# Where tiles lie in SBUF: the streamed operands of each stage moved down behind the weights, x and the small tiles moved to the upper end

## The chip, the cores and the metric

The kernel runs on one core of one Trainium2 chip. The metric is the device time of one execution in microseconds (us). Three executions of the kernel before gave 2356.27, 2360.15 and 2360.02, with a median of 2360.02.

## What is computed

512 tokens of 1024 features in float32 go through two blocks. Cut to what matters (`x` is carried through all of it, each line with its own weights):

```python
x = x + 0.5 * ffn(rms_norm(x))           # swiglu: (silu(h @ Wg) * (h @ Wu)) @ Wo, 1024 -> 2816 -> 1024
x = x + mixer1(rms_norm(x)) @ Wmo        # band attention and sparse attention, heads of 64
x = x + 0.5 * ffn(rms_norm(x))           # a second swiglu
x = x + mixer2(rms_norm(x))              # GLA (4 heads) and retention (4 heads), each with an output
                                         # projection ya or yb, then one more projection
x = x + moe(rms_norm(x))                 # 32 experts of float32 weights, 64 places each; RMS norm at the end
```

## The kernel before

The activations are kept transposed: eight tiles of 128 features x 512 tokens. The five stages run one after the other in one program: `ffn`, `mixer1`, `ffn`, `mixer2`, `moe`.

**The large matmuls.** Up to the experts every large product is made of three matmuls in float32r. Each operand is split into a high and a low part: ACT makes the high part (line 84), DVE the low part (line 85). `mm3` then adds high·high (line 99), high weight·low activation (line 100) and low weight·high activation (line 101) into one PSUM tile. In `gemm` the weight part is the stationary operand (loaded by LDWEIGHTS as 128x128) and the activation part is the moving operand, 128x512, streamed from SBUF through the array. A trace row such as `po<-hh,whi` reads: PSUM tile po, moving hh, stationary whi. The exception is `vv`, in which the weights whi and wlo are the moving operand.

**What is streamed where.** The names are needed below:
- `xh`, `xl`: the parts of the normalised x, moving in all projections `pg`, `pu` (ffn) and `pj` (mixers). At the end of mixer2 the same places are used again for `oh`, `ol`, which move in the last projection, also called `po` in rows.
- `hh`, `hl`: the parts of the hidden tiles of `ffn`, moving in `po`. `ffn` goes through the 22 hidden tiles in three parts of 8, 7 and 7 (PARTS). In each part `pg` and `pu` of every hidden tile are made and then eight `po` sums over the part's tiles: 24 x (8 + 7 + 7) = 528 matmuls of po in each ffn.
- `fh`, `fl`: the parts of a half of mixer2's heads, moving in `ya` (GLA) and `yb` (retention).
- `mh`, `ml`: the parts of the second half of mixer1's result, moving in mixer1's `po`.
- `th`, `tlo`: the parts of transposed attention weights, moving in mixer1's `pv`; `sh`, `sl` and `rh`, `rl` do the like for short sums of mixer2 (`pvo`, `rs`).
- `wexp`: float32 weights of the experts, moving in the experts' `pg`, `pu`, `pd`. They are held in a ring of 21 places at the upper end of SBUF, in the places of wraw, whi and wlo (`EXTRA`), and in a few late ones.

**What sets the order of the work.** The code is issued in program order on each engine. `load_w` puts each weight tile on SP's DMA queue (line 91) into one of three `wraw` places; a DMA whose place is still in use waits in that queue, and whatever is queued behind it on SP waits too. Which earlier instruction a new tile has to wait for is set by the place: a tile waits for the last users of the places that it covers. So moving a pool can move a wait even when no operation changes.

**Where tiles lie.** Pools are stacked from the lower end (left) and from the upper end (right). Before, the left side holds const, wraw, whi, wlo, xhl (xh and xl), `small`, then x, and behind x the pools of the stage. All parts of SBUF below are given per partition.

Of the kernel before, what the change touches and what calls it, by code (L numbers as in the profile page):

```python
# [10 lines left out]
F32R = mybir.dt.float32r  # L11
# [24 lines left out]
def ap_of(t, offset, dims):  # L36
    return bass.AP(tensor=t.tensor, offset=t.offset + offset, ap=dims)


class Kern:  # L40
    def __init__(self, ctx, tc, A, out, dbg=None, stop=None):
        self.ctx, self.tc, self.nc, self.A, self.out = ctx, tc, tc.nc, A, out
        self.dbg = dbg or {}
        self.stop = stop
        self.sin = None
        e = ctx.enter_context
        self.const = e(tc.tile_pool(name="const", bufs=1))
        self.wp = e(tc.tile_pool(name="wts", bufs=1))
        self.xp = e(tc.tile_pool(name="xhl", bufs=1))
        self.sm = e(tc.tile_pool(name="small", bufs=2))  # L50
        self.dram = e(tc.tile_pool(name="dram", bufs=1, space=bass.MemoryType.DRAM))
        self.ps = e(tc.tile_pool(name="psum", bufs=1, space=PSUM))
        self.xd = self.dram.tile([128, DT, 512], F32, name="xd")
# [2 lines left out]
        return self.tc.alloc_tile_pool(name=name, bufs=bufs, side=side, reuse_waits="tile")  # L56

    def open_x(self):
        self.xpool = self.pool("x")
        self.x = [self.xpool.tile([128, 512], F32, name=f"x{t}") for t in range(DT)]  # L60

    def spill(self, t):
# [148 lines left out]
    def ffn(self, w_in, w_out, nxt, aside=()):  # L211
        nc, A, X = self.nc, self.A, self.X
        aside = list(aside)
        if True:
            fp = self.pool("ffn")
            for pi, (n0, cnt) in enumerate(PARTS):
                if pi == len(PARTS) - 1 and nxt is not None:
                    nxt = nxt()
                H = []
                for n in range(n0, n0 + cnt):  # L220
                    if n != 1:
                        wg, self.first = self.first or self.load_w(A[w_in][:, n, 0]), None
                        pg = self.acc("pg")
                    wu = self.load_w(A[w_in][:, n, 1])
                    if n == 1:
                        pg = pg1
                        pu = self.ps.tile([128, 512], F32, name="pu", tag="lg", bufs=2)
                    else:
                        self.gemm(pg, wg, X, DT)
                        pu = self.acc("pu")  # L230
                    if n == 0:

                        self.gemm(pu, wu, X, DT)
                        wg, pg1 = self.load_w(A[w_in][:, 1, 0]), self.acc("pg")
                        self.gemm(pg1, wg, X, DT, range(4))
                        self.norm_end()
                        self.gemm(pg1, wg, X, DT, range(4, DT))
                    if n >= 3 and aside:
                        aside.pop(0)()
                    g = fp.tile([128, 512], F32, name="g", bufs=2)  # L240
                    nc.vector.tensor_tensor(out=g, in0=pg, in1=self.rstd, op=OP.mult)
                    nc.scalar.activation(g, g, AF.Silu)
                    if n:
                        self.gemm(pu, wu, X, DT)
                    u = fp.tile([128, 512], F32, name="u", bufs=2)
                    nc.vector.tensor_tensor(out=u, in0=pu, in1=self.rstd, op=OP.mult)
                    h = fp.tile([128, 512], F32, name="h", bufs=2)
                    nc.vector.tensor_tensor(out=h, in0=g, in1=u, op=OP.mult)
                    hh = fp.tile([128, 512], F32R, name="hh", bufs=10)
                    hl = fp.tile([128, 512], F32R, name="hl", bufs=10)  # L250
                    self.split(h, hh, hl)
                    H.append((hh, hl))
                for n in range(DT):
                    w = self.load_w(A[w_out][:, n, n0 * 128:(n0 + cnt) * 128])
                    po = self.acc("po")
                    self.gemm(po, w, H, cnt)
                    nc.vector.scalar_tensor_tensor(self.x[n], po, 0.5, self.x[n], op0=OP.mult, op1=OP.add)
                    if pi == len(PARTS) - 1 and nxt is not None:
                        nxt(n)
            fp.release()  # L260


    def bias_lines(self):
# [387 lines left out]
    def mixer1(self, nxt):  # L651
        nc, A = self.nc, self.A
        self.xpool.release()
        mp = self.mp = self.pool("mixp")
        self.ms = self.pool("mixs", 2)
        mw = self.mw = self.pool("mixw", 2)
        self.sk = mp.tile([128, 2, 8], F32, name="sk")
        nc.sync.dma_start(self.sk[:, 0], ap_of(A["sinks"], 0, [[0, 128], [1, 8]]))
        nc.vector.tensor_scalar(self.sk[:, 1], self.sk[:, 0], -1.0, None, op0=OP.mult)
        self.mix = mp.tile([128, DT, 512], F32, name="mix")  # L660
        self.qs = ([], [])
        self.pvq = []
        ps = self.proj(4)
        self.norm_end(tokens=True)
        pq = [self.proj(n) for n in range(2)]
        self.ka = self.k_tile(4, "k_norm_a", "ka", ps)
        for n in range(2):
            self.q_tile(n, "q_norm_a", self.qs[0], pq[n])
        self.values()
        qt = lambda l, n: (lambda: self.q_tile(n, "q_norm_" + "ab"[l], self.qs[l]))  # L670

        def kt(name, n):
            return lambda: setattr(self, name, self.k_tile(n, "k_norm_b", name))
        self.pipeline(self.band_units(0) + self.band_units(1),
                      [lambda: self.compress_in(0), qt(0, 2), qt(0, 3), lambda: self.compress_hidden(0),
                       lambda: self.compress_in(1), kt("ksel", 11), qt(1, 5), lambda: self.compress_hidden(1),
                       qt(1, 6), self.compress_out])
        self.kwin = self.k_tile(12, "k_norm_b", "kwin")
        no = lambda: None
        self.pipeline(self.nsa_units(0) + self.nsa_units(1),  # L680
                      [no, qt(1, 7), no, no, qt(1, 8), no, self.first_parts, no] +
                      [f for n in range(DT) for f in (no, lambda n=n: self.first_half(n))])
        mw.release()
        self.ms.release()
        mo = self.pool("mo", side="right")
        M = []
        for t in range(4, DT):
            h = mo.tile([128, 512], F32R, name=f"mh{t}")
            lo = mo.tile([128, 512], F32R, name=f"ml{t}")
            self.split(self.mix[:, t], h, lo)  # L690
            M.append((h, lo))
        mp.release()
        self.open_x()
        nxt = nxt and nxt()
        for n in range(DT):
            w = self.load_w(A["wmo"][:, n, 512:1024])
            po = self.acc("po")
            self.gemm(po, w, M, 4)
            nc.vector.tensor_tensor(out=self.x[n], in0=po, in1=self.half[n], op=OP.add)
            if nxt:  # L700
                nxt(n)
        mo.release()
# [92 lines left out]
    def head_out(self, V, c0, nt, sh, sl, wname, w0, gates, wait):  # L795
# [22 lines left out]
        def rest():  # L818
            p = self.ps.tile([128, 512], F32, name="on", tag="pv", bufs=1)
            nc.tensor.matmul(p, self.ones, ssum, start=True, stop=True)  # L820
            r = self.rstd_from(p, 1.0 / (128 * nt), "hr", None)
            for t in range(nt):
                g = gates[t]
                nc.gpsimd.tensor_tensor(out=g, in0=g, in1=r, op=OP.mult)
                o = O[t]
                nc.vector.scalar_tensor_tensor(o, o, self.vcol(wname, w0 + t), g, op0=OP.mult, op1=OP.mult)
                fh = self.m2.tile([128, 512], F32R, name="fh", bufs=8)
                fl = self.m2.tile([128, 512], F32R, name="fl", bufs=8)
                self.split(o, fh, fl)
                F.append((fh, fl))  # L830
        self.pend = [wait, rest]
# [166 lines left out]
    def mixer2(self):  # L998
        nc, A = self.nc, self.A
        self.xpool.release()  # L1000
        self.m2 = self.pool("m2")
        m3 = self.m3 = self.pool("gla")
        self.gmask = m3.tile([128, 8, 128], I32, name="gmask")
# [69 lines left out]
                M.append((h, lo))  # L1073
        sp.release()
        self.m2.release()
        self.moe_open()
        self.open_x()
        self.route_open()
# [712 lines left out]
```

## Time and profile before

| | |
|---|---|
| three runs, median | 2356.27, 2360.15, 2360.02; 2360.02 us |
| profiled execution, time and span | 2363.39 us, 2361.6 us |
| granted TensorE clock, mean | 0.986 |
| PE busy | 2288.4 us (97%) |
| DVE, ACT, POOL busy | 1150.5, 857.1, 402.6 us |
| DMA | 390.83 MB, mean 165 GB/s |

One execution is profiled; its time and the span (first to last instruction) differ by 1.8 us. Matmuls are pipelined and their ends are modelled: a record of 0.39 us may begin every 0.23 us. So the pace of a run of matmuls is read from the starts: the start of the first of a run, the start of the instruction behind the run, and the count between them.

### The profile page before, as it was taken

What the parts mean: (1) busy time and instruction counts of PE and PEld (TensorE: products, weight loads), DVE (VectorE), ACT (ScalarE), POOL (GpSimd) and SP (SyncE); (2) the same over time, 40 slices, a digit from 0 to 9 for tenths busy, and PEclk for the clock granted to TensorE, in tenths of its full rate; (3) what the DMA queues carried; (4) which work ended last, traced back from release to release, by engine and by line L of the source; (5) the groups of instructions that cost most, each with busy time, mean ns of one, the idle gap of its engine ahead of it and who ended that gap; (6) DMA issues with size and microseconds to landing.
All of it is one profiled execution on the core that took longest, in us unless ns stands there. A gap on an engine that the chain in (4) does not pass through costs nothing.

```text
span 2361.6 us, 27737 instructions
## 1 busy us (share of the span) xinstructions
PE 2288.4 (97%) x10344; PEld 1678.2 (71%) x10344; DVE 1150.5 (49%) x2074; ACT 857.1 (36%) x1441; POOL 402.6 (17%) x408
## 2 busy tenths in 40 slices
PE   8999999999999999999999999999999899999997
PEld 6888888776788888877877887787878544444443
DVE  4534345878754344457674445435454333322223
ACT  4222235677642222354444354334553211100002
POOL 1000002335310000014340121203113201110101
PEclk9999999999999999999999999999999899999999
DMA  5533335221143333332213322232237999999997
GB/s 157 176 97 92 98 104 155 90 63 49 42 121 95 97 91 99 119 112 63 72 59 110 105 85 87 87 109 67 88 117 226 356 389 408 406 407 407 404 408 303
DMA packets 126099, 390.83 MB, mean 165 GB/s; under 512 B 15399, under 2 KB 21072, under 8 KB 125705
## 3 DMA queue, kind: packets, MB, share of 16 engines
q1 hardware_dynamic: 121064, 380.10, 47.1%
q10 hardware_dynamic: 2592, 4.72, 0.5%
q0 software_dynamic: 2304, 4.20, 0.5%
q8 instruction: 83, 1.36, 0.2%
q14 instruction: 56, 0.45, 0.1%
HBM read 378.44 MB, written 17.33 MB: 168 GB/s over the span
## 4 chain that ended last, share of the span: by engine, by line
PE 85%; DVE 6%; DMA 4%; ACT 3%; issue 1%; POOL 1%; SPq 0%; POOLq 0%; DVEq 0%; ACTq 0%
PE pg L1335 5%; PE pj L101 5%; PE pj L100 5%; PE pj L99 5%; PE pu L1335 5%; PE po L100 4%; PE po L101 4%; PE po L99 4%; PE pd L1335 4%; PE pu L101 3%; PE pu L100 3%; PE pu L99 3%; PE pg L100 3%; PE pg L101 3%; PE pg L99 3%; PE py L1402 2%
## 5 line engine op out<-in xcount | busy, mean ns | idle before, releaser
L84 ACT ACTIVATE whi<-wraw 128x1024 fp32r<-128x1024 f32 (+2 forms) x290 | 296.2, 1021 | 711.5 <-issue 190.8
L85 DVE TENSOR_TENSOR wlo<-wraw,whi 128x1024 fp32r<-128x1024 f32 (+2 forms) x282 | 347.2, 1231 | 141.2 <-ACT whi L84 135.7
L101 PE MATMUL pj<-xh,wlo 128*128 128x512 f32 x624 | 248.5, 398 | 10.4 <-DVE wlo L85 10.4
L99 PE MATMUL pj<-xh,whi 128*128 128x512 f32 x624 | 251.8, 403 | 0.0
L100 PE MATMUL pj<-xl,whi 128*128 128x512 f32 x624 | 247.4, 396 | 0.0
L157 POOL TENSOR_TENSOR ssq<-ssq,sq 128x512 f32<-128x512 f32 x34 | 52.7, 1549 | 770.4 <-ACT sq L154 768.3
L1335 PE MATMUL pg<-wexp,xs 128*64 128x512 f32 x474 | 164.6, 608 | 2.3 <-DMA wexp<-in_wexp 2.3
L1335 PE MATMUL pu<-wexp,xs 128*64 128x512 f32 x474 | 160.4, 593 | 0.0
L99 PE MATMUL pg<-xh,whi 128*128 128x512 f32 x352 | 139.2, 395 | 7.0 <-ACT xh L142 7.0
L101 PEld LDWEIGHTS pj<-xh,wlo 128*128 128x128 f32 x624 | 119.2, 191 | 36.3 <-DVE wlo L85 12.1
L100 PE MATMUL po<-hl,whi 128*128 128x512 f32 x352 | 139.6, 397 | 0.0
L99 PE MATMUL po<-hh,whi 128*128 128x512 f32 x352 | 139.5, 396 | 0.0
L101 PE MATMUL po<-hh,wlo 128*128 128x512 f32 x352 | 139.5, 396 | 0.0
L100 PE MATMUL pg<-xl,whi 128*128 128x512 f32 x352 | 138.3, 393 | 0.5 <-DVE xl L143 0.5
L101 PE MATMUL pu<-xh,wlo 128*128 128x512 f32 x352 | 137.2, 390 | 1.6 <-DVE wlo L85 1.6
L101 PE MATMUL pg<-xh,wlo 128*128 128x512 f32 x352 | 138.1, 392 | 0.0
L99 PEld LDWEIGHTS pj<-xh,whi 128*128 128x128 f32 x624 | 119.3, 191 | 25.9 <-issue 2.6
L100 PEld LDWEIGHTS pj<-xl,whi 128*128 128x128 f32 x624 | 119.3, 191 | 25.0 <-issue 1.7
L99 PE MATMUL pu<-xh,whi 128*128 128x512 f32 x352 | 137.1, 389 | 0.0
L100 PE MATMUL pu<-xl,whi 128*128 128x512 f32 x352 | 137.0, 389 | 0.0
L1335 PE MATMUL pd<-wexp,hs 128*64 128x512 f32 x484 | 115.7, 599 | 0.0
L1335 PEld LDWEIGHTS pu<-wexp,xs 128*64 128x64 f32 x474 | 49.0, 138 | 78.8 <-issue 78.2
(613 smaller groups left out, 4420.2 us busy)
## 6 DMA issues: line engine op xcount, KB each, us to landing
wexp<-in_wexp SPq DMA_DIRECT2D x358, 512.0 KB
wraw<-in_w1i SPq DMA_DIRECT2D x44, 512.0 KB
wraw<-in_w2i SPq DMA_DIRECT2D x44, 512.0 KB
wraw<-in_wr SPq DMA_DIRECT2D x32, 512.0 KB
wpark<-in_wexp SPq DMA_DIRECT2D x48, 256.0 KB
wraw<-in_wg SPq DMA_DIRECT2D x16, 512.0 KB
wraw<-in_wrv SPq DMA_DIRECT2D x16, 512.0 KB
wraw<-in_wbr SPq DMA_DIRECT2D x16, 512.0 KB
```

What stands on the lines that cost most here:

```text
L84: return (self.nc.scalar.activation(hi, src, AF.Copy), (eng or self.nc.vector).tensor_tensor(out=lo, in0=src, in1=hi.bitcast(F32), op=OP.s ...
L85: (eng or self.nc.vector).tensor_tensor(out=lo, in0=src, in1=hi.bitcast(F32), op=OP.subtract))
L99: mm(ps, ah, bh, start=first, stop=False)
L100: mm(ps, ah, bl, start=False, stop=False)
L101: mm(ps, al, bh, start=False, stop=last)
L157: self.nc.gpsimd.tensor_tensor(out=self.ssq, in0=self.ssq, in1=sq, op=OP.add)
L1335: self.pe(self.nc.tensor.matmul(out[r], x[:, r], self.loaded[2 * p + j, c][half], start=first, stop=last))
L1402: self.pe(nc.tensor.matmul(ps, oh[:, i * 128:i * 128 + 128], y[:, hf * 512:hf * 512 + 512], start=(first and j == 0), stop=(j == 1)))
```

## The change

No operation is added, removed or given another shape. Pools change sides, and two new pools come in:
- `small` and `x` go to the right side (x just below small in ffn and mixer1, and below the experts' ring in moe).
- `hid`, new, holds hh and hl right behind xhl; the other tiles of ffn follow behind it.
- `m2f`, new, holds fh and fl right behind xhl; the other pools of mixer2 follow.
- In mixer1 x is opened before `mo`, so that mh and ml lie below x on the right.

```diff
-        self.sm = e(tc.tile_pool(name="small", bufs=2))
+        self.sm = e(tc.tile_pool(name="small", bufs=2, side="right"))
...
-        self.xpool = self.pool("x")
+        self.xpool = self.pool("x", side="right")
...
+            hp = self.pool("hid")
             fp = self.pool("ffn")
...
-                    hh = fp.tile([128, 512], F32R, name="hh", bufs=10)
-                    hl = fp.tile([128, 512], F32R, name="hl", bufs=10)
+                    hh = hp.tile([128, 512], F32R, name="hh", bufs=10)
+                    hl = hp.tile([128, 512], F32R, name="hl", bufs=10)
...
             fp.release()
+            hp.release()
...
         self.ms.release()
+        self.open_x()
         mo = self.pool("mo", side="right")
...
         mp.release()
-        self.open_x()
...
-                fh = self.m2.tile([128, 512], F32R, name="fh", bufs=8)
-                fl = self.m2.tile([128, 512], F32R, name="fl", bufs=8)
+                fh = self.m2f.tile([128, 512], F32R, name="fh", bufs=8)
+                fl = self.m2f.tile([128, 512], F32R, name="fl", bufs=8)
...
         self.xpool.release()
+        self.m2f = self.pool("m2f")
         self.m2 = self.pool("m2")
...
         self.m2.release()
+        self.m2f.release()
```

The start addresses that follow from it, as the two programs are laid out (KiB in a partition, first to last start of the tiles; the remainder is that of the start in bytes by 64):

| tiles | before | remainder | after | remainder |
|---|---|---|---|---|
| whi, wlo (stationary; moving in vv) | 29.9 to 41.9 | 0 | the same | 0 |
| xh, xl, oh, ol | 45.9 to 75.9 | 0 | the same | 0 |
| hh, hl | 118.6 to 156.6 | 32 | 77.9 to 115.9 | 0 |
| fh, fl | 150.6 to 180.6 | 32 | 77.9 to 107.9 | 0 |
| mh, ml | 208.0 to 222.0 | 32 | 179.3 to 193.3 | 0 |
| th, tlo | 207.8 to 217.8 | 0 | 195.1 to 205.1 | 32 |
| sh, sl | 122.6 and 130.6 | 32 | 141.9 and 149.9 | 0 |
| x (ffn, mixer1) | 90.6 to 104.6 | 32 | 195.3 to 209.3 | 0 |
| experts' ring (wexp) | 140.0 to 220.0 | 32 | 127.3 to 207.3 | 0 |

The order of instructions on PE, ACT, DVE and POOL is all but the same. On SP two places differ.

First SP's queue from the end of the first ffn into mixer1. `sk` and `bA` are small tables that mixer1's softmax reads, `wmv` the weights of vv. Before:

```order
L91 DMA wraw<-in_w1o 128x896 x8
L91 DMA wraw<-in_wmi 128x1024 x3
L91 DMA wraw<-in_wmv 128x816 x2
L658 DMA sk<-in_sinks 128x8
L299 DMA bA<-d2A 128x256 x4
L480 DMA cw_2992<-in_cw 128x512
L91 DMA wraw<-in_wmv 128x816
```

The same place with the change:

```order
L91 DMA wraw<-in_w1o 128x896 x8
L91 DMA wraw<-in_wmi 128x1024 x3
L91 DMA wraw<-in_wmv 128x816
L660 DMA sk<-in_sinks 128x8
L301 DMA bA<-d2A 128x256 x4
L91 DMA wraw<-in_wmv 128x816
L482 DMA cw_2996<-in_cw 128x512
```

The load of sk and the four of bA move one weight load earlier; sk now covers a place of hh and waits for the last po that reads it, where it waited for a transfer of x out of SBUF.

Second SP's queue around the second ffn and the start of mixer2. `gmask` (512 KB) and `gup` (32 KB) are tables of mixer2; gup is the stationary operand of the matmul pz. Before they stand among the first weight loads of the second ffn (w2i):

```order
L91 DMA wraw<-in_wmo 128x512 x6
L91 DMA wraw<-in_w2i 128x1024 x4
L1004 DMA gmask<-in_gmask 128x1024
L91 DMA wraw<-in_w2i 128x1024
L850 DMA gup<-in_gup 16x512
L91 DMA wraw<-in_w2i 128x1024 x11
```

With the change, at the start of mixer2:

```order
L91 DMA wraw<-in_w2o 128x896
L91 DMA wraw<-in_wgd 128x1024
L91 DMA wraw<-in_wgv 128x1024 x4
L1007 DMA gmask<-in_gmask 128x1024
L852 DMA gup<-in_gup 16x512
L91 DMA wraw<-in_wg 128x1024 x12
```

Both tables now wait for the end of the second ffn, whose hidden tiles lie where they go, and are queued behind mixer2's first five weight loads. One more wait moves: one load of expert weights into a late place, which now covers tiles of the router, waits for the router's matmul pc (line 1229).

## Rows read from the trace of the kernel before

**Rows 1.** The page: busy time of PE, granted clock, GB/s in 40 slices

```profile
PE 2288.4 (97%) x10344; PEld 1678.2 (71%) x10344; DVE 1150.5 (49%) x2074; ACT 857.1 (36%) x1441; POOL 402.6 (17%) x408
...
PEclk9999999999999999999999999999999899999999
...
GB/s 157 176 97 92 98 104 155 90 63 49 42 121 95 97 91 99 119 112 63 72 59 110 105 85 87 87 109 67 88 117 226 356 389 408 406 407 407 404 408 303
```

**Rows 2.** Timeline of PE, end of ffn's first part: start, duration (us), engine, line

```profile
97.78 0.39 PE L99 MATMUL pu<-xh,whi 128*128 128x512 f32 x1
...
103.22 0.40 PE L99 MATMUL po<-hh,whi 128*128 128x512 f32 x1
...
148.20 0.40 PE L99 MATMUL pg<-xh,whi 128*128 128x512 f32 x1
```

**Rows 3.** Windows: stretch, length, busy us per engine, PEclk, DMA share, GB/s

```profile
97.78:103.22 5.44, 5.44 (x25) 4.50 (x24) 1.92 (x2) 1.58 (x2) 0.00 (x0) 1.00 0.39 119
103.22:148.20 44.98, 44.98 (x194) 36.16 (x192) 16.54 (x18) 9.16 (x10) 0.00 (x0) 1.00 0.32 94
...
1900.00:2300.00 400.00, 397.10 (x1727) 170.59 (x1724) 117.84 (x295) 41.51 (x81) 44.93 (x64) 1.00 1.03 405
```

**Rows 4.** Timeline of PE in mixer2: ya, pj, and the last projection

```profile
1266.15 0.40 PE L99 MATMUL ya<-fh,whi 128*128 128x512 f32 x1
...
1271.76 0.40 PE L99 MATMUL pj<-xh,whi 128*128 128x512 f32 x1
...
1277.21 0.40 PE L99 MATMUL ya<-fh,whi 128*128 128x512 f32 x1
...
1803.71 0.39 PE L99 MATMUL po<-oh,whi 128*128 128x512 f32 x1
...
1808.48 0.39 PE L99 MATMUL po<-oh,whi 128*128 128x512 f32 x1
```

**Rows 5.** Timeline of PE, mixer1's last projection, 24 matmuls apart

```profile
642.16 0.39 PE L99 MATMUL po<-mh,whi 128*128 128x512 f32 x1
...
647.76 0.39 PE L99 MATMUL po<-mh,whi 128*128 128x512 f32 x1
```

**Rows 6.** Tile views of po, ya, yb, mh: counts, ns min/median/max, starts

```profile
L99 PE MATMUL po<-hh,whi x352: 392/397/400, 103.2 to 1022.3; 128*128 128x512 f32 x176
...
L99 PE MATMUL ya<-fh,whi x64: 391/398/628, 1230.5 to 1326.4; 128*128 128x512 f32 x64
...
L99 PE MATMUL yb<-fh,whi x128: 388/397/628, 1500.6 to 1797.1; 128*128 128x512 f32 x128
...
L99 PE MATMUL po<-mh,whi x32: 393/396/632, 634.3 to 658.3; 128*128 128x512 f32 x32
```

**Rows 7.** Timeline of PE in vv: weights move, 12 matmuls between rows

```profile
401.47 0.35 PE L99 MATMUL vv<-whi,xh 128*128 128x408 f32 x1
...
403.71 0.34 PE L99 MATMUL vv<-whi,xh 128*128 128x408 f32 x1
...
405.92 0.35 PE L99 MATMUL vv<-whi,xh 128*128 128x408 f32 x1
```

**Rows 8.** Tile view of pv: moving th

```profile
L379 PE MATMUL pv<-th,V x54: 388/474/802, 435.5 to 631.3; 128*128 128x512 f32 x54
```

**Rows 9.** Timeline at the start of mixer1: DVE's last x, SP's load of sk

```profile
379.52 0.69 DVE L257 SCALAR_TENSOR_TENSOR x<-po,x 128x512 f32<-128x512 f32 x1 [2.12 <-PE po L101]
...
382.06 0.42 SPq L658 DMA_DIRECT2D sk<-in_sinks  x1
```

**Rows 10.** Timeline at the start of mixer2: SP's weight loads, PE's first pz

```profile
1010.32 15.34 SPq L91 DMA_DIRECT2D wraw<-in_wgv  x4
...
1032.54 1.12 PE L856 MATMUL pz<-gdn,gup 16*128 16x512 f32 x2
```

**Rows 11.** Timeline at the start of moe: PE's pc, SP's next expert load

```profile
1861.83 0.80 PE L1229 MATMUL pc<-M,before 128*128 128x32 f32 x3
...
1863.99 1.61 SPq L1110 DMA_DIRECT2D wexp<-in_wexp  x2
```

## The prediction

> **What bounds the kernel now.** [...] Up to the experts no other resource comes near: in a stretch of 192 po matmuls DVE is busy 16.54 of 44.98 us, ACT 9.16, and DMA runs at 94 GB/s [rows 3]. There the time is the number of matmuls times the pace at which they start. From about 1900 us on it is otherwise: 405 GB/s, a DMA share at its top and PE busy 397.10 of 400 us, so transfer and matmul are both near their limit [rows 3]. So I looked for the pace of a matmul in each stage, in the timeline of PE, by the starts.
>
> All float32r matmuls of 512 columns should take one pace. They do not. At the end of ffn's first part 24 matmuls that move xh and xl go from 97.78 to 103.22, 5.44 us or 226.7 ns each; the 192 behind them, which move hh and hl, go from 103.22 to 148.20, 44.98 us or 234.3 ns each [rows 2]. Both stretches have the granted clock 1.00 [rows 3]. In mixer2 the two paces stand next to each other again: 24 of ya (fh and fl) in 5.61 us, 233.8 ns, then 24 of pj (xh and xl) in 5.45 us, 227.1 ns [rows 4]. The difference is 7.6 ns for each matmul (234.3 - 226.7).
>
> What sets it? Not the form or the output: the last projection po moves oh and ol, which lie in the places of xh and xl, by the same helper, and starts 21 in 4.77 us, 227.1 ns [rows 4]. Not other engines' traffic: DVE and ACT together are busy 64% of the fast stretch (3.50 of 5.44 us), 57% of the slow one [rows 3]. What is left is where the moving tile lies. The fast ones begin at 46 to 76 KiB with the remainder 0 by 64 bytes, the slow ones at 119 to 181 KiB with the remainder 32. One pair of rows holds the position fixed: vv moves halves of whi and wlo, and the second half begins 1632 bytes behind the first, which is a remainder of 32. Twelve matmuls of 408 columns on the second half take 2.24 us (186.7 ns), twelve on the first 2.21 us (184.2 ns) [rows 7]. So the remainder alone costs something at a low address, 2.5 ns on 408 columns or by length 3.1 on 512, less than the 7.6. The rest can be the position, or a remainder that costs more with another stationary operand; the trace cannot part them. The change moves hh, hl, fh and fl in both: down to 78 to 116 KiB and to remainder 0.
>
> **The change, part by part.** The gain is counted in matmuls:
> - po of both ffn: 3 x 352 = 1056 [rows 6] x 7.6 ns = 8.0 us.
> - ya and yb: 3 x (64 + 128) = 576 [rows 6] x 7.6 = 4.4 us. A few of them begin in stretches at half clock (the maximum of 628 ns against a median of 397), where the gain may not show; that is some tenths of a us at most.
> - mixer1's last projection: mh and ml get remainder 0 but stay high, at 179 to 193 KiB. 24 take 5.60 us now, 233.3 ns [rows 5], 6.6 over the fast pace; 96 matmuls [rows 6] could win 0 to 0.6 us. I take 0.6, since the remainder is the only thing here that is seen to cost.
> - th and tlo go the other way, from remainder 0 to 32. Their matmuls come in short bursts (median 474 ns on th [rows 8]), so no pace can be read; 2 x (54 + 8) = 124 at 0 to 7.6 ns is a loss of 0 to 0.9 us. sh, sl, rh, rl in short sums of mixer2 get remainder 0 and could win about as much. I take nothing for both.
>
> PE gets faster by 3% in these stretches, and the work that feeds it must keep up: with DVE at 37% and 94 GB/s [rows 3] it does. Moved small tiles and x cost nothing for ACT, DVE and POOL, which have that cover; without it they would have to become slower by more than half to be seen.
>
> Moved waits. In SP's queue at the start of mixer1, sk now waits for the last po that reads hh. That po is done before DVE adds it into x at 379.52, and sk is issued at 382.06 today [rows 9], so the wait is over before sk's turn, and what is queued behind it (bA, cw, the wmv loads) is not held. At the start of mixer2, gmask and gup go behind the four wgv loads, which leave SP's queue by 1025.66 (1010.32 + 15.34); gup is wanted by pz on PE at 1032.54 [rows 10]. In front of gup lie up to 512 KB of the last wgv and 512 KB of gmask, 2.6 us at 405 GB/s [rows 3], so it lands from 1028.3 on; with as much again for issue and the way it would be 1030.9. That leaves 1.6 to 4.2 us: nothing on PE. The wg loads behind it start about 0.8 us later and wait for a place in any case. Were gup late, PE would stand, and the loss is bounded by a us or two. The expert load that now waits for pc is issued at 1863.99; pc's three matmuls end about 1862.6 [rows 11]: nothing, and with some 1.4 us of cover.
>
> In the experts' stage nothing is shorter: the ring moves from 140 to 127 KiB, and the same bytes go in at the same 405 GB/s. It starts earlier by what was won before and ends earlier by the same.
>
> The sum: 8.0 + 4.4 + 0.6 = 13.0 us. The profiled execution took 2363.39 us, 3.4 above the median of the runs shown; 13.0 less is 2350.4, and against the median 2347.0. I predict 2347.
>
> [...] The rows above show a pace that differs by 7.6 ns with the place of the moving tile [rows 2, 4]. [...]
>
> **The rivals.**
> - *Only the nearest tiles become fast* (a border in position rather than the remainder). The fast rows end at 78 KiB. If the border lies near 98 KiB, hh (704 matmuls) and fh (384) win and hl and fl do not: 1088 x 7.6 ns = 8.3 us, 2351.7. For it: the remainder at a low place costs only 3.1 of the 7.6. Against it: hh at 119 and fl at 167 KiB and more give the same 234 [rows 2, 4], so nothing in the trace grows with distance.
> - *No change*: the pace belongs to something that does not move with the pools, for example a border just above 78 KiB, or a pairing of moving and stationary tile. It gives 2360. For it: the two differ in the operand as well as in place, and mh at 208 KiB pays the same as hh [rows 2, 5], which fits "behind xhl" as well as any remainder. Against it: the oh rows and the vv rows.
> - *Slower*: the experts' stage is at the limit of its transfers, and the ring's new addresses take them less well, or transfers and faster neighbours meet. The stage lasts some 490 us from 1864 to the end; each per cent is 4.9 us. It eats the 13.0 us when the rate falls by 2.7%, from 405 to under 395 GB/s, and makes the kernel slower by over 0.2% under about 391. At 4% it would be 2360 - 13 + 19.6 = 2367. Against it: the rate stays within 404 to 408 GB/s for seven slices [rows 1] although the ring's places and the low places of the weights take turns.
>
> **Chances and range.** 0.2%, or 4.7 us, is about what a measurement of this kernel can tell from no change. Full gain 0.58, with its own range 2344.5 to 2350 (the median of before may lie 2 us elsewhere; th and sh count up to 1 us each way); nearest tiles only 0.13; no change 0.20; slower 0.09. Of the partial case nearly all is over 0.2% faster, so faster 0.70, within 0.2% 0.21, slower 0.09. A range that leaves out no more than 2 in 10 has to reach from the full gain to no change: 2344.5 to 2360.5.
>
> **What would show it.** In the profile of the changed kernel ffn's po in a part of eight should take 43.5 us for 192 matmuls (226.7 each) in place of 44.98, 24 of ya 5.44 us, 192 of yb 43.5. Po with hh fast and hl slow, alternating, would be the first rival; 44.98 again the second. mh at 5.44 for 24 would say that the remainder decides, at 5.60 the position. The experts' stage should last as long as before at 405 GB/s. gup late would show as idle time of PE before pz at line 858. I am wrong if po keeps its 234 ns, or if the experts' stage gets longer than what the stages before it give.

## The result and the profile after

Five runs of the changed kernel gave 2345.84 to 2351.43 us, median 2347.77; five of the kernel before 2356.27 to 2362.06, median 2360.15. The ratio is 0.9945, with a 95% interval from 0.9933 to 0.9957: faster by 0.55%. The medians lie 12.4 us apart. The prediction was 2347.0.

The profiled execution has a span of 2344.0 us, 17.6 less than before; the page's first part, and its rows on the clock and the bytes:

```profile
span 2344.0 us, 27722 instructions
...
PE 2272.5 (97%) x10344; PEld 1674.3 (71%) x10344; DVE 1151.0 (49%) x2074; ACT 856.7 (37%) x1441; POOL 402.7 (17%) x408
...
PEclk9999999999999999999999999999999899999999
...
GB/s 168 172 94 93 104 100 162 84 61 50 45 113 99 91 98 99 117 118 63 72 60 111 106 83 83 88 113 69 89 125 229 363 398 407 406 407 406 406 408 304
```

Against [rows 1] PE has lost 15.9 us of busy time with the same number of instructions, DVE, ACT and POOL nothing. The timeline of PE at the places of [rows 2, 4]: the end of ffn's first part, then ya and pj in mixer2:

```profile
101.44 0.39 PE L99 MATMUL po<-hh,whi 128*128 128x512 f32 x1
...
144.96 0.39 PE L99 MATMUL pg<-xh,whi 128*128 128x512 f32 x1
...
1256.30 0.39 PE L99 MATMUL ya<-fh,whi 128*128 128x512 f32 x1
...
1261.74 0.39 PE L99 MATMUL pj<-xh,whi 128*128 128x512 f32 x1
...
1267.18 0.39 PE L99 MATMUL ya<-fh,whi 128*128 128x512 f32 x1
```

192 of po take 43.52 us (44.98 before), and 24 of ya take 5.44, as 24 of pj do. So po and ya now start every 226.7 ns, as the matmuls on xh and xl do. The second yb took 44.98 us before, in the timeline of PE from its first matmul to the po behind it:

```profile
1752.81 0.40 PE L99 MATMUL yb<-fh,whi 128*128 128x512 f32 x1
...
1797.79 0.40 PE L99 MATMUL po<-oh,whi 128*128 128x512 f32 x1
```

With the change, the windows of the po stretch, of the second yb (1738.69 to 1782.21) and of 400 us of the experts' stage:

```profile
101.44:144.96 43.52, 43.52 (x194) 36.04 (x192) 16.54 (x18) 9.16 (x10) 0.00 (x0) 1.00 0.33 97
1738.69:1782.21 43.52, 43.52 (x194) 36.04 (x192) 25.08 (x31) 15.34 (x20) 14.99 (x7) 1.00 0.50 156
1883.00:2283.00 400.00, 397.39 (x1730) 170.73 (x1727) 117.74 (x295) 41.43 (x81) 44.79 (x64) 1.00 1.03 406
```

Against [rows 3] DVE and ACT do the same work beside the po stretch, and the experts' stage runs at 406 GB/s (405 before). One term did not come. mixer1's last projection, 24 matmuls apart:

```profile
635.33 0.39 PE L99 MATMUL po<-mh,whi 128*128 128x512 f32 x1
...
640.93 0.39 PE L99 MATMUL po<-mh,whi 128*128 128x512 f32 x1
```

5.60 us, as in [rows 5], although mh and ml now begin at a multiple of 64 bytes.

### The profile page after: what moved, and what is told of

The parts are those of the page before. It is cut to its first block, busy times and chain, and to the rows that moved or that the text cites. A ratio compares the mean times of both kernels' runs of the same rounds, so it can differ in the third digit from the quotient of the medians.

```text
span 2344.0 us, 27722 instructions
## 1 busy us (share of the span) xinstructions
PE 2272.5 (97%) x10344; PEld 1674.3 (71%) x10344; DVE 1151.0 (49%) x2074; ACT 856.7 (37%) x1441; POOL 402.7 (17%) x408
## 4 chain that ended last, share of the span: by engine, by line
PE 87%; DVE 5%; DMA 3%; ACT 3%; POOL 1%; issue 1%; SPq 0%; POOLq 0%; DVEq 0%; ACTq 0%
PE pg L1339 5%; PE pj L101 5%; PE pj L99 5%; PE pj L100 5%; PE pu L1339 5%; PE po L100 4%; PE po L101 4%; PE po L99 4%; PE pd L1339 4%; PE pu L101 3%; PE pu L99 3%; PE pu L100 3%; PE pg L100 3%; PE pg L101 3%; PE pg L99 3%; PE py L1406 2%
## 5 line engine op out<-in xcount | busy, mean ns | idle before, releaser
L101 PE MATMUL pj<-xh,wlo 128*128 128x512 f32 x624 | 247.4, 397 | 10.3 <-DVE wlo L85 10.3
L99 PE MATMUL pj<-xh,whi 128*128 128x512 f32 x624 | 250.7, 402 | 0.0
L99 PE MATMUL pg<-xh,whi 128*128 128x512 f32 x352 | 139.1, 395 | 6.7 <-ACT xh L142 6.7
L101 PEld LDWEIGHTS pj<-xh,wlo 128*128 128x128 f32 x624 | 118.5, 190 | 36.2 <-DVE wlo L85 12.0
L101 PE MATMUL pg<-xh,wlo 128*128 128x512 f32 x352 | 138.1, 392 | 0.0
L101 PE MATMUL pu<-xh,wlo 128*128 128x512 f32 x352 | 137.1, 389 | 0.4 <-DVE wlo L85 0.4
L99 PE MATMUL pu<-xh,whi 128*128 128x512 f32 x352 | 137.1, 389 | 0.0
L99 PE MATMUL po<-hh,whi 128*128 128x512 f32 x352 | 137.0, 389 | 0.0
L101 PE MATMUL po<-hh,wlo 128*128 128x512 f32 x352 | 136.9, 389 | 0.0
L99 PEld LDWEIGHTS pj<-xh,whi 128*128 128x128 f32 x624 | 118.8, 190 | 25.4 <-issue 2.6
```

The lines of the kernel that those rows point to most:

```text
L99: mm(ps, ah, bh, start=first, stop=False)
L101: mm(ps, al, bh, start=False, stop=last)
```

## The experiments

The result says that the place of the streamed tiles is worth some 12 us, but not what in the place: the change moved them down and onto another remainder at once. Four kernels part the two. Theory A is the remainder of the moving tile by 64 bytes, theory B its position. Each kernel's time stands beside its ratio to the kernel before, run on the same chip.

**The kernel before, 32 bytes behind the small tiles** (high, remainder 0):

```diff
         self.sm = e(tc.tile_pool(name="small", bufs=2))
+        pad = e(tc.tile_pool(name="pad", bufs=1)).tile([128, 8], F32, name="pad")
+        self.nc.vector.memset(pad, 0.0)
```

> The kernel before with 32 unused bytes behind the small tiles: hh, hl, fh and fl stay high (119 to 182 KiB) and get the remainder 0 by 64 bytes. Theory A, the remainder of the moving tile sets the pace: po, ya and yb start every 226.7 ns (192 of po in 43.5 us), and the time is that of the changed kernel, some 12.4 us under the kernel before (2347.8). Theory B, the position sets it (mh in the changed kernel still takes 233 ns at 179 to 193 KiB with the remainder 0): 234 ns stay, 192 of po in 45.0 us, and the time is that of the kernel before within 3 us (2360).

Measured: 2359.32, ratio 0.9997 (0.9988 to 1.0005). The timeline of PE, first po of a part of eight and the instruction behind the last (a pad opened above mm3 adds two lines, so that here and below its first line is L101 where it was L99):

```profile
102.66 0.39 PE L101 MATMUL po<-hh,whi 128*128 128x512 f32 x1
...
147.46 0.39 PE L101 MATMUL pg<-xh,whi 128*128 128x512 f32 x1
```

44.80 us, 233.3 ns: theory A falls, at least as "by 64".

**The changed kernel, the same 32 bytes ahead of hid and m2f** (low, remainder 32); the pad stands behind the line that opens `small`, as above.

> The changed kernel with 32 unused bytes ahead of hid and m2f: hh, hl, fh and fl stay low (78 to 118 KiB) and get the remainder 32 again. Theory A, the remainder: 234 ns come back, 192 of po in 45.0 us, and the time is that of the kernel before (2360). Theory B, the position: 226.7 ns stay, 43.5 us, and the time is that of the changed kernel within 3 us (2347.8). A third outcome, some 230 ns and 2354, would say that each has a part.

Measured: 2358.13, ratio 0.9993 (0.9984 to 1.0002). In the timeline of PE 192 of po go from 102.60 to 147.40:

```profile
102.60 0.40 PE L101 MATMUL po<-hh,whi 128*128 128x512 f32 x1
...
147.40 0.40 PE L101 MATMUL pg<-xh,whi 128*128 128x512 f32 x1
```

44.80 us at 78 to 118 KiB: 32 bytes take the gain away, and theory B falls too.

**The changed kernel without hid and m2f** (small and x on the right alone; fh at 138 to 168 KiB):

```diff
-            hp = self.pool("hid")
...
-                    hh = hp.tile([128, 512], F32R, name="hh", bufs=10)
+                    hh = fp.tile([128, 512], F32R, name="hh", bufs=10)
...
-                fh = self.m2f.tile([128, 512], F32R, name="fh", bufs=8)
+                fh = self.m2.tile([128, 512], F32R, name="fh", bufs=8)
```

> The changed kernel without the pools hid and m2f (small and x on the right alone): hh at 90 to 110, hl at 110 to 130, fh and fl at 138 to 170 KiB, all with the remainder 0. Theory A, the remainder: all of po, ya and yb at 227 ns, the time of the changed kernel (2347.8). Theory B, the position, with a border between 118 and 119 KiB: hh fast, hl above 118 slow (about half of its 352 matmuls, 1.3 us), ya and yb slow at 234 ns (4.4 us): 2353.5.

Measured: 2346.55, ratio 0.9943 (0.9931 to 0.9956), all of the gain. The timeline of PE at the second yb:

```profile
1742.68 0.39 PE L99 MATMUL yb<-fh,whi 128*128 128x512 f32 x1
...
1786.20 0.39 PE L99 MATMUL po<-oh,whi 128*128 128x512 f32 x1
```

43.52 us for 192 with fh and fl high. So neither the new pools nor the low place is needed.

**The kernel before with hid and m2f alone** (small and x stay on the left; the same lines the other way round).

> The kernel before with the pools hid and m2f alone (small and x stay low): hh at 107 to 127, hl at 127 to 147, fh at 91 to 107, fl at 107 to 123 KiB, all with the remainder 32. Theory A, the remainder: all at 234 ns, the time of the kernel before (2360). Theory B, the position, with a border between 118 and 119 KiB: fh fast, hh and fl fast below the border, the rest slow, about 850 of 1632 matmuls at 7.6 ns less, 6.5 us: 2353.6.

Measured: 2359.14, ratio 0.9996 (0.9986 to 1.0006). 192 of po take 44.98 us, of yb 44.97, with fh down at 91 KiB. The two new pools are worth nothing by themselves.

What do the tiles that take 226.7 ns share? Set against the start of the stationary tile (whi and wlo begin at 448 modulo 512 bytes, and a slice of 128 columns is 512 bytes further), their starts are 0 bytes off modulo 512; those of the tiles that take 233 or 234 ns are 160 (before; mh there 32), 192 (first run), 32 (second run) and, for mh in the changed kernel, 384 bytes off. The second half of a wmv tile in vv is 96 off [rows 7]. This gives theory C, the difference between the starts of moving and stationary tile, and as its rival theory D, the moving tile's own address. Tiles whose difference is 0 are called in step below.

**Everything on the left up by 32 bytes together:**

```diff
         self.const = e(tc.tile_pool(name="const", bufs=1))
+        pad = e(tc.tile_pool(name="pad", bufs=1)).tile([128, 8], F32, name="pad")
+        self.nc.vector.memset(pad[:, 0:8], 0.0)
```

> The changed kernel with 32 unused bytes at the lower end, ahead of the weights: weights, xh/xl, hh/hl and fh/fl all move up by 32 bytes together, so that their starts modulo 512 are 480 instead of 448 and their differences stay 0. Theory C, the difference between the starts of the moving and the stationary tile modulo 512 (or a divisor of it) sets the pace, 0 being fast: pg, pu, pj, po, ya and yb all stay at 226.8 ns, the time is that of the changed kernel (2347 within 3). Theory D, the address of the moving tile itself: all of them become slow, some 5800 matmuls at about 7 ns more, 41 us: 2388.

Measured: 2346.45, ratio 0.9943 (0.9927 to 0.9960). In the timeline of PE, po of the first part and pg and pu of the third begin and end at

```profile
102.90 0.39 PE L101 MATMUL po<-hh,whi 128*128 128x512 f32 x1
...
146.42 0.39 PE L101 MATMUL pg<-xh,whi 128*128 128x512 f32 x1
...
260.68 0.39 PE L101 MATMUL pg<-xh,whi 128*128 128x512 f32 x1
...
336.84 0.39 PE L101 MATMUL po<-hh,whi 128*128 128x512 f32 x1
```

43.52 us for 192 and 76.16 for 336, 226.7 ns each. Nothing became slower: theory D falls, C stands. The comparison with the second run is even closer. hh, hl, fh and fl lie here at the very addresses that they had there, where 192 of po took 44.80 us; only the weights lay 32 bytes lower. mh and ml, on the right, do not move and are 96 off the weights here, 24 matmuls apart:

```profile
640.19 0.40 PE L101 MATMUL po<-mh,whi 128*128 128x512 f32 x1
...
645.79 0.40 PE L101 MATMUL po<-mh,whi 128*128 128x512 f32 x1
```

That is 5.60 us, 233.3 ns.

**xh and xl 64 bytes off the weights, hh and hl 128 off in the first ffn and 256 in the second, fh and fl 512:**

```diff
         self.wp = e(tc.tile_pool(name="wts", bufs=1))
+        pad = e(tc.tile_pool(name="pad", bufs=1)).tile([128, 16], F32, name="pad")
...
+            self.nffn = getattr(self, "nffn", 0) + 1
+            npad = (64, 192)[self.nffn - 1]
+            pp = self.pool("hpad") if npad else None
...
+        mpad = self.pool("mpad")
+        t = mpad.tile([128, 112], F32, name="mpad")
```

> The changed kernel with unused bytes between the tiles: xh and xl begin 64 bytes off the weights' step (modulo 512), hh and hl 128 off in the first ffn and 256 off in the second, fh and fl 512 off, which is 0 again. Theory C, the difference to the stationary tile: pg, pu, pj, the last po and also vv, in which the weights move and xh is stationary, become slow (233 ns); po of the first ffn is slow, of the second slow if the period is 512 and fast if it is 256; ya and yb stay at 227. Some 4900 matmuls at 6.6 ns more, 32 us, and po 3.5 to 7: 2380 to 2387. Theory D, the address of the moving tile alone: the same, but vv, whose moving tile has not moved, stays at 226.9 ns.

Measured: 2360.92, ratio 1.0003 (0.9994 to 1.0013): 14 us above the run just told, where 32 and more were expected. The timeline of PE has po of the first ffn, pg and pu of its third part, po of the second ffn, and 24 of vv:

```profile
103.31 0.39 PE L101 MATMUL po<-hh,whi 128*128 128x512 f32 x1
...
147.92 0.39 PE L101 MATMUL pg<-xh,whi 128*128 128x512 f32 x1
...
263.87 0.40 PE L101 MATMUL pg<-xh,whi 128*128 128x512 f32 x1
...
340.79 0.40 PE L101 MATMUL po<-hh,whi 128*128 128x512 f32 x1
...
747.40 0.39 PE L101 MATMUL po<-hh,whi 128*128 128x512 f32 x1
...
790.93 0.40 PE L101 MATMUL pg<-xh,whi 128*128 128x512 f32 x1
...
1360.50 0.39 PE L101 MATMUL vv<-whi,xh 128*128 128x512 f32 x1
...
1366.10 0.39 PE L101 MATMUL vv<-whi,xh 128*128 128x512 f32 x1
```

At 128 off 192 matmuls take 44.61 us (232.3 ns each), at 256 off 43.53 (226.7): the period is 256 bytes, not 512. At 64 off 336 take 76.92 (228.9 ns), so 64 costs only a third of the rest in pg and pu, which is why the time came out low. But pj does not keep one pace at the same 64. Its five stretches of 96 directly behind vv run at 233.3 ns, the others at 229 to 230; one of the five, from the timeline of PE:

```profile
1371.70 0.40 PE L101 MATMUL pj<-xh,whi 128*128 128x512 f32 x1
...
1394.10 0.40 PE L101 MATMUL rs<-rh 128*128 128x512 f32 x1
```

These 96 take 22.40 us, and the 96 of pj just ahead of that vv, from 1327.31 to 1349.31, take 22.00. So at 64 off the difference alone does not set the pace: the 96 behind vv take 0.40 us more than the 96 ahead of it, and no run shows why. And vv becomes slow: 24 in 5.60 us, 233.3 ns, where the changed kernel takes 5.44. Its moving tiles, whi and wlo, lie where they lay; xh, which is stationary there, has moved. That is the difference, seen from the other side.

**hh and hl 224 and 288 bytes off, fh and fl 480** (the same pads, of 224, 288 and 480 bytes):

> The changed kernel with hh and hl 224 bytes off the weights' step in the first ffn and 288 bytes in the second, fh and fl 480 bytes off. Theories C and D: all slow, 233 ns, with a period of 256 or 512; if the loss grows with the distance from the nearest step, 480 (32 below a step) costs least. Time that of the kernel before, 2360, in either case.

Measured, one run: 2359.42. 192 matmuls take 44.80 us at 224, 44.81 at 288 and 44.80 at 480 (the second yb), 233.3 ns each. 288 is 32 and 480 is 224 modulo 256, and both agree with the runs at 32 and 224: the loss does not grow with the distance from a step.

**384 bytes on the right, so that mh is in step at 179 to 193 KiB:**

```diff
         self.sm = e(tc.tile_pool(name="small", bufs=2, side="right"))
+        rpad = e(tc.tile_pool(name="rpad", bufs=1, side="right")).tile([128, 96], F32, name="rpad")
```

> The changed kernel with 384 unused bytes on the right below the small tiles, so that mh and ml, still at 179 to 193 KiB, begin on the weights' step (448 modulo 512); hh, hl, fh and fl as in the changed kernel. Theory C (or D): the 96 matmuls on mh and ml go from 233 to 227 ns, 24 of them 5.44 us in place of 5.60. Theory B, the position: 233 ns stay. The time is that of the changed kernel less 0.6 us, which cannot be told from it.

Measured: 2346.51, ratio 0.9948 (0.9931 to 0.9964), as the changed kernel. The timeline of PE, 24 matmuls apart:

```profile
638.15 0.39 PE L101 MATMUL po<-mh,whi 128*128 128x512 f32 x1
...
643.59 0.39 PE L101 MATMUL po<-mh,whi 128*128 128x512 f32 x1
```

5.44 us: the missing term comes when the difference is a multiple of 256, at the upper end of SBUF. (The whole stretch of 96 takes 24.99 us all the same, 24.59 in the changed kernel, because more of its first matmuls start 427 ns apart. Those of the changed kernel that do, from 629.64 to 631.35, have a granted clock of 0.50.)

**xh and xl 32 bytes off, all else 256:** a pad of 32 bytes behind the weights and 224 ahead of hid and m2f.

> The changed kernel with xh and xl 32 bytes off the weights' step, and hh, hl, fh, fl 256 bytes off it. Theory C with a period of 256 bytes: po, ya and yb keep 226.8 ns, and pg, pu, pj, the last po, poa and vv (weights moving, 224 off) go to 233.4 ns: some 4850 matmuls at 6.6 ns, 32 us more than the changed kernel, 2379 within 4; slower than the kernel before by 0.8%. If the loss is not the difference between the two starts, 2347 (nothing) or some value between.

Measured: 2373.72, ratio 1.0062 (1.0045 to 1.0079), slower than before. In the timeline of PE 336 of pg and pu go from 264.80 to 343.20:

```profile
104.66 0.40 PE L101 MATMUL po<-hh,whi 128*128 128x512 f32 x1
...
148.22 0.40 PE L101 MATMUL pg<-xh,whi 128*128 128x512 f32 x1
...
264.80 0.40 PE L101 MATMUL pg<-xh,whi 128*128 128x512 f32 x1
...
343.20 0.40 PE L101 MATMUL po<-hh,whi 128*128 128x512 f32 x1
```

78.40 us, 233.3 ns as expected, and po at 256 off stays at 43.56. xh and xl lie here at the addresses that they had with everything on the left up by 32 bytes, where the same 336 took 76.16 us; only the weights differ. The total is 27 us above the 2347 of the kernels in step, not 32. In stretches where PE often waits for other engines the profile shows less than their share: 255.41 us against 253.80 in the changed kernel from the end of the first ffn to mixer1's last projection, 198.53 against 199.26 from pz to the first ya, there with a mean clock of 0.98 against 0.97. So a shift of 32 bytes is worth over 1% of this kernel.

**Half of each stationary tile loaded**, in the kernel before and in the changed one:

```diff
-                    self.gemm(po, w, H, cnt)
+                    for k in range(cnt):
+                        c = slice(k * 128, k * 128 + 64)
+                        self.mm3(po[0:64], w[0][:, c], w[1][:, c], H[k][0], H[k][1], k == 0, k == cnt - 1)
```

> The kernel before, with po of both ffn loading and computing only the first 64 of each 128 output features (the other half of ffn's output is left out). It asks whether the loss is made while the next stationary tile is loaded beside the moving one. Theory C1, the two reads meet: half the load, so half the loss, some 230.5 ns for a matmul of po in place of 234.3 with hh and hl still 160 bytes off. Theory C2, the loss belongs to the moving stream and its own stationary tile: 234.3 ns stay. Theory C3, a shorter load no longer meets it: 226.8 ns.

> The changed kernel, with po of both ffn loading and computing only the first 64 of each 128 output features (the other half of ffn's output is left out): the control for the run before. All theories: 226.8 ns for a matmul of po, as with whole tiles; if it is less, the load costs something at difference 0 too.

Measured, one run each: 2360.1 and 2352.45. The timelines of PE, first of the kernel before with half tiles, then of the changed kernel with half tiles:

```profile
103.21 0.39 PE L99 MATMUL po<-hh,whi 128*64 128x512 f32 x1
...
147.64 0.39 PE L99 MATMUL pg<-xh,whi 128*128 128x512 f32 x1
```

```profile
101.67 0.40 PE L99 MATMUL po<-hh,whi 128*64 128x512 f32 x1
...
145.83 0.39 PE L99 MATMUL pg<-xh,whi 128*128 128x512 f32 x1
```

160 off, 192 matmuls take 44.43 us, 231.4 ns; that alone would have fitted theory C1. But the control was not the 226.8 that all theories expected: in step it takes 44.16, 230.0 ns. With half tiles the two paces nearly meet, one down by 2.9, the other up by 3.3. Nor is 231.4 the only pace at 160 off. In the third part of the first ffn, behind a short wait of PE for hl, 148 of po run at the 226.8 of theory C3:

```profile
343.61 0.40 PE L101 MATMUL po<-hh,wlo 128*64 128x512 f32 x1
...
377.18 0.39 PE L99 MATMUL pj<-xh,whi 128*128 128x512 f32 x1
```

That is 33.57 us; the other five stretches keep 231.4, and with whole tiles the same wait leaves 234.3. So with half tiles, as at 64 off, the difference alone does not set the pace. The width of the stationary tile is party to it, but the edit halves the rows of the output together with the load, so that it is the load is not shown, and no run settles theory C1.

## Why the prediction was right

**The main terms held.** The traces of before and after give each stretch between the same two matmuls. The six po stretches give back 1.46, 1.25, 1.09, 1.46, 1.27 and 1.25 us, 7.8 where 8.0 was forecast. ya and yb, from the first to the last ya and over the two yb stretches, give 1.63, 1.18 and 1.46, 4.3 where 4.4 was. Together 12.1 of the 12.4 us between the medians.

**The step that failed is "what sets it".** It named the position or the remainder by 64 of the moving tile, and said that the trace could not part them. It is neither: the runs show the difference between the starts of moving and stationary tile, modulo 256 bytes: with whole tiles and 512 columns 0 is fast, and every other value tried is slower. That the sum came out all the same was luck: behind the weights every tile up to xl7 is a multiple of 2 KiB long, so whatever starts there has not only the remainder 0 by 64 but is in step; and with small and x gone from the left, hh, hl, fh and fl are, with or without pools of their own. The prediction's own sign, mh at 5.60 for the position, pointed the wrong way too. The pair of rows from vv that carried the remainder [rows 7] was a real effect with another meaning: 1632 bytes are 96 off modulo 256. Its scaling by length to 3.1 ns was too small: 96 off with 512 columns costs 6.6 (mh with everything on the left up by 32 bytes).

**mh was mis-sized by the same error:** 0.6 forecast, 0.09 measured over the whole stretch (24.68 to 24.59), since its difference is 128 modulo 256. In step it does reach 5.44 for 24. That mh paid the same as hh before, as the prediction has it, is not quite so either: 233.3 ns at 32 off, 234.3 at 160.

**The rivals.** The border near 98 KiB fell with the first profile: hh and hl share one pace (192 of po on both in 43.52 us). No change had "a pairing of moving and stationary tile" for its reason. The pairing is what there is, but it moves with the pools, so it spoke for the gain. Slower needed the experts' stage under 395 GB/s; it ran at 406. DVE's load did not move the pace: in the windows above po and yb take the same 43.52 us beside 16.54 and 25.08 us of DVE. The places of PE's own two operands did, by up to 7.6 ns a matmul (226.7 to 234.3).

**The moved waits cost nothing that counts.** The timeline of SP and PE at the start of mixer2, after:

```profile
1014.86 0.42 SPq L1007 DMA_DIRECT2D gmask<-in_gmask  x1
1015.38 0.39 SPq L852 DMA_DIRECT2D gup<-in_gup  x1
...
1021.93 0.69 PE L858 MATMUL pz<-gdn,gup 16*128 16x512 f32 x1
```

gup is issued 6.6 us ahead of pz, and the stretch from the end of ffn to pz is 9.81 us against 9.58: 0.2 us. sk is issued at 373.25, before the first ffn ends, and holds nothing.

**The profile's 17.6 us.** The rest over 12.1 is not from these matmuls. It sits in the stretches between them and has both signs. From pz to the first ya the changed kernel takes 1.3 us more, because the granted clock fell just behind pz, to 0.50 from 1025 to 1031; the windows of 13 us there, after (mean clock 0.74) and before (1.00):

```profile
1022.00:1035.00 13.00, 13.00 (x35) 8.21 (x36) 9.54 (x21) 8.19 (x13) 1.49 (x2) 0.74 0.06 24
```

```profile
1033.00:1046.00 13.00, 12.85 (x49) 8.66 (x48) 11.06 (x23) 8.94 (x14) 1.49 (x2) 1.00 0.05 21
```

In the other kernels this stretch takes 197.7 to 198.1 or 199.2 to 199.3 us, in layouts of either pace (but for the two that shift xh itself and the two with half tiles). The larger part, 2.7 us between the two yb, goes with the clock as well. The windows of that stretch, before and after:

```profile
1552.00:1752.81 200.81, 194.19 (x869) 159.87 (x868) 101.89 (x126) 101.87 (x158) 40.77 (x28) 0.97 0.30 90
```

```profile
1540.58:1738.69 198.11, 191.50 (x870) 157.97 (x868) 101.84 (x126) 101.87 (x158) 40.74 (x28) 0.99 0.31 91
```

The mean clock is 0.97 before and 0.99 after. All kernels in step have 0.99 and 198.1 to 198.3 us here, but so has the kernel in which 32 bytes had undone the gain (198.35); the one with hh 224 off has 0.97 and 200.96. That the layout has no part in this clock is not shown. The median of the runs is the better measure, and the profiled execution of the changed kernel was its fastest of five.

## What to carry to other kernels

Where PE bounds a stage, read the pace of its matmuls from their starts and compare stages with the same shape: two paces under one clock are a lead. For float32r matmuls of 512 columns with a new stationary tile each time, let the tile that is streamed and the tile that is loaded begin a multiple of 256 bytes apart in a partition (226.7 ns at 0 and at 256 here, 228.9 to 234.3 at the other distances tried); an odd small tile between them is enough to lose it (the 32 bytes of the second run took the ratio from 0.9945 to 0.9993). Before crediting a layout with nearness or a pool of its own, shift it by 32 bytes.

## What was not expected of the hardware

The pace of a float32r matmul of 512 columns with a new stationary tile each time, by the difference of the two starts modulo 256 bytes, in this study: 226.7 ns at 0, 233.3 at 32, 228.9 to 233.3 at 64, 233.3 at 96, 232.3 to 233.3 at 128, 234.3 at 160, 233.3 at 192 and at 224. 0 is as fast at 179 as at 78 KiB. With the weights as the moving operand 24 of vv took 5.44 us at 0 and 5.60 at 192. All slices of the weights lie in one step, so the runs do not tell whether the stationary tile that counts is the matmul's own or the next one, which is loaded meanwhile (PEld is busy 36.04 of the 43.52 us of the po stretch, PE all of it). With a stationary tile of half the width it is 230.0 at 0 and 226.8 or 231.4 at 160. With 408 columns the loss is smaller: 184.2 at 0 and 186.7 at 96 [rows 7], and at 32 off, in the run with xh 64 off, twelve from 402.24 to 404.44 take 2.20 us, 183.4 ns, no loss at all. What makes the loss stays open.
